# The first down-projection of each feed-forward part moves into the fixed-order region of its round

## The chip, the core and the metric

The kernel runs on one core of a Trainium2 chip. The metric is device time in microseconds (us), as the median of several executions; lower is better. The core has a matrix engine (TensorE, called PE in the profile, with PEld for its weight loads), a vector engine (VectorE, DVE), an activation engine (ScalarE, ACT), GpSimd (POOL), a queue engine that starts transfers (SyncE, SP), and 16 DMA engines. Matrix products accumulate in PSUM, which the kernel uses as eight banks of 128x512 f32. Each engine takes its own instructions in the order in which the program has them, and waits on semaphores for the others.

## The reference

Two layers, each of four parts on a residual stream h of 512 tokens by 1024 channels. The feed-forward part is there twice in a layer, so four times in all:

```
for l in range(DEPTH):                                   # DEPTH = 2
    h = h + 0.5 * swiglu(rms_norm(h, ffn1_norm[l]), w_gate, w_up, w_down)   # first feed-forward part
    h = h + hybrid_mixer(rms_norm(h, mix_norm[l]), ...)  # recurrent + window attention + DeltaNet
    h = h + 0.5 * swiglu(rms_norm(h, ffn2_norm[l]), ...) # second feed-forward part
    h = h + sigmoid(rms_norm(h, ple_norm[l]) @ w_ple_gate[l]) * (p[l] @ w_ple_proj[l])
return rms_norm(h, final_norm)

swiglu(x) = (silu(x @ w_gate) * (x @ w_up)) @ w_down     # 1024 -> 2816 -> 1024
```

All is float32. The change touches the product with w_down, and nothing of what is computed.

## The kernel before, in words

Float32 accuracy is made from three reduced-precision products: every operand is split into a high and a low half, and mm3 (L142 to L145) issues high x high, high x low and low x high as three matmuls of one accumulation. The split of a weight tile (L122 to L125 for down-projection weights, L429 and L434 for gate and up weights) is one ACT instruction that rounds to the high half (gh, wh or sh) and one DVE instruction that subtracts it from the raw tile to get the low half (gl, wl or sl). So each weight tile passes through a DMA on SP's queue into a raw buffer wr (three of them, used in rotation), then ACT, then DVE, then PE.

A feed-forward part is the generator `ffn`. The 2816 hidden channels are 22 blocks of 128, handled as 11 pairs; a pair has a gate unit and an up unit, each a Strassen-like scheme of seven products (class Unit, products p(1) to p(7), L466). Work is in two rounds (ROUNDS): pairs 0 to 4, then 5 to 10. At the end of a round the hidden blocks it made are multiplied with w_down. In round 0 (r == 0) this is the first down-projection: for each of eight output blocks d, `chunk(d)` loads and splits eight of its ten weight blocks, `down` issues 24 matmuls with them, and `end(d)` issues six more with the last two blocks, whose weights `make_end(e)` loads and splits for two values of d at a time, followed by `residual(d)`: two DVE instructions, L566 (dt, scaled from PSUM) and L567 (hT, added to the residual stream). At d = 6 the weights of the first unit of round 1 are prepared too: `pipe[2 * j1].whole()`, which is splits a, b, d, c with the sums s2 (L440) and s4 (L446) between them.

Who sets the order: PE runs in the order of the code everywhere (L73). Inside `with tc.manual_schedule(engines=inner)` (L680, one region in each round), ACT and DVE too run in the order of the code. Outside it, a scheduler with a model of the engines places ACT, DVE and POOL instructions. It may put an instruction ahead of others, also of those of a region before it. SP's transfers and the order of GpSimd follow the scheduler in both versions.

In the kernel before, the units of round 0 are in the region (L680 to L777) and the first down-projection (`if r == 0:`, L779 on) is outside.

Of the kernel before, what the change touches and what calls it, by code (L numbers as in the profile page):

```python
# [19 lines left out]
S = 512  # L20
D = 1024
KD = 8
# [36 lines left out]
def trunk(ctx: ExitStack, tc: tile.TileContext, a):  # L59
# [9 lines left out]
    def bank(shape, name):  # L69
        return banks.tile(shape, F32, tag="b", name=name)  # L70
# [52 lines left out]
    def split(x, hi, lo):  # L123
        A.activation(out=hi, in_=x, func=AF.Copy)  # L124
        V.tensor_tensor(out=lo, in0=x, in1=hi.bitcast(F32), op=ALU.subtract)  # L125
# [16 lines left out]
    def mm3(out, wh, wl, xh, xl, start, stop):  # L142
        T.matmul(out=out, lhsT=wh, rhs=xh, start=start, stop=False)  # L143
        T.matmul(out=out, lhsT=wh, rhs=xl, start=False, stop=False)  # L144
        T.matmul(out=out, lhsT=wl, rhs=xh, start=False, stop=stop)  # L145
# [206 lines left out]
    def ffn(l, which):  # L352
        with ExitStack() as es:
# [23 lines left out]
            def halfgroup():  # L377
                return [fp.tile([128, 4, 128], F32R, tag=t, name=t, bufs=2) for t in ("sh", "sl")]

            def loaded(src, k):  # L380
                raw = wrp.tile([128, k, 128], F32, tag="wr", name="wr")
                nc.sync.dma_start(out=raw, in_=src)
                return raw

            def grouped(raw, k):
                w = group(k, 128)
                split(raw, *w)
                return w


            def load(u):
                j, m = units[u]
                src = a[f"{m}{which}"][l, j]
                if u not in raw1:
                    raw1[u] = loaded(src[:, 0:8], 8)
                    raw3[u] = wrp.tile([128, 8, 128], F32, tag="wr", name="wr")
                    nc.sync.dma_start(out=raw3[u][:, 0:4], in_=src[:, 12:16])

            def load2(u):
                if u < len(units) and u not in raw2:  # L400
                    j, m = units[u]
                    src = a[f"{m}{which}"][l, j]
                    r2 = raw2[u] = fp.tile([128, 8, 128], F32, tag="r2", name="r2", bufs=3)
                    nc.sync.dma_start(out=r2, in_=src[:, 4:12])
                    G.dma_start(out=r2.rearrange("p k n -> p (k n)"), in_=src[:, 8:16].rearrange("p k n -> p (k n)"),
                                accum_op=ALU.add)
# [152 lines left out]
            def down(pd, w, ws, fs, start, stop):  # L559
                for i, f in zip(ws, fs):  # L560
                    h, l_ = (t[:, f % 2, :] for t in hidden[f // 2])
                    mm3(pd, w[0][:, i, :], w[1][:, i, :], h, l_, start and f == fs[0], stop and f == fs[-1])

            def residual(d, pd):
                dt = ft.tile([128, S], F32, tag="ys", name="dt", bufs=2)
                V.scalar_tensor_tensor(out=dt, in0=pd, scalar=0.5, in1=norm.rb, op0=ALU.mult, op1=ALU.mult)  # L566
                V.tensor_tensor(out=hT[:, d, :], in0=hT[:, d, :], in1=dt, op=ALU.add)  # L567
# [3 lines left out]
            pipe = {}  # L571
# [90 lines left out]
            for r, (j0, j1) in enumerate(ROUNDS):  # L662
# [4 lines left out]
                def chunk(d):  # L667
                    if d not in made:
                        made[d] = grouped(loaded(src[l, d][:, t0:t0 + 8, :], 8), 8)
                    return made[d]  # L670

                def make_end(e):
                    raw = wrp.tile([128, 4, 128], F32, tag="wr", name="wr")
                    for i in range(2):
                        nc.sync.dma_start(out=raw[:, 2 * i:2 * i + 2, :], in_=src[l, 2 * e + i][:, 8:10, :])
                    ends[e] = halfgroup()
                    split(raw, *ends[e])

                made, ends = {}, {}
# [96 lines left out]
                    pair.hi()  # L776
                    pair.lo()  # L777

                if r == 0:  # L779
                    def end(d):  # L780
                        e = d // 2
                        if e not in ends:
                            make_end(e)
                        i = 2 * (d % 2)
                        down(pds[d], ends[e], (i, i + 1), (8, 9), False, True)
                        residual(d, pds[d])

                    pds = {}
                    for d in range(KD):
                        pds[d] = bank([128, S], "pd")  # L790
                        chunk(d)
                        if d + 1 < KD:
                            chunk(d + 1)
                        if d == KD - 2:
                            load2(2 * j1)
                            load(2 * j1)
                            pipe[2 * j1] = Weights(2 * j1)
                            pipe[2 * j1].whole()
                        down(pds[d], chunk(d), range(8), range(8), True, False)
                        if d == 0:  # L800
                            continue
                        for e in ((0, 1) if d == 1 else (d,)):
                            end(e)
            pds = []
            for d in range(KD):
                pds.append(bank([128, S], "pd"))
# [796 lines left out]
    norm = Norm(par[:, 0, C_F1:C_F1 + 8], True)  # L1603

    f = ffn(0, 1)
    next(f)
    norm.ps = bank([128, NT, 2], "ssc")
# [18 lines left out]
    for l in range(L):  # L1626
        pl = par[:, l, :]
        norm = rest(f, norm, pl[:, C_MX:C_MX + 8])
        f = ffn(l, 2)
        norm = mixer(l, norm, pl[:, C_F2:C_F2 + 8], f)  # L1630
        norm = rest(f, norm, pl[:, C_PL:C_PL + 8])
        f = ffn(l + 1, 1) if l + 1 < L else None
        norm = ple(l, norm, par[:, l + 1, C_F1:C_F1 + 8] if f else None, f)
# [123 lines left out]
```

## Time and profile before

| what | value |
|---|---|
| median of 3 runs | 2035.08 us (2030.96 to 2036.78) |
| the profiled execution, device time | 2031.3 us |
| its span, first to last instruction | 2029.4 us |
| PE busy | 1978.0 us (97%) |
| DVE, ACT, POOL busy | 1492.6, 980.8, 169.5 us |
| mean granted clock of TensorE | 0.986 |

The profile is of one execution. Busy times are of instructions, so an engine that waits is not busy. The times in rows are microseconds from the start of the span. A row of the timeline has the start, the length (overlapping neighbours in a pipelined engine, so that starts are closer than lengths), the engine, the line of the kernel, the operation, output and inputs, the shape, and in square brackets the idle time before it and what ended it. The granted clock is a share: 1.00 is 2.4 GHz, 0.50 is 1.2 GHz. The names: pd is a PSUM bank of the down-projection, pg, pu, qg and qu are banks of the gate and up units, ys, e, cg, cu and th are temporaries of a unit and its gating, h0h and h0l are the halves of the fifth hidden pair of the round.

### The profile page before, as it was taken

The numbers are of one execution on the slowest core, as the hardware profiler recorded it, in microseconds if no ns is written. First come the engines' busy times: TensorE is split into PE (matmuls) and PEld (weight loads), VectorE is DVE, ScalarE is ACT, GpSimd is POOL, SyncE is SP. The second block draws the span as 40 slices with busy tenths as digits, with TensorE's granted clock in tenths as the row PEclk, the third lists the DMA queues.
The fourth block names the chain that finished last, engine by engine and source line by source line (L and its number), as shares of the span: only waits on it lengthen the run. The fifth ranks groups of instructions, "written<-read, shape, count | busy, mean of one in ns | idle before, by whom it ended". The sixth has DMA issues, their size and how long they took to land.

```text
span 2029.4 us, 32039 instructions
## 1 busy us (share of the span) xinstructions
PE 1978.0 (97%) x12657; PEld 1760.0 (87%) x12657; DVE 1492.6 (74%) x2591; ACT 980.8 (48%) x1629; POOL 169.5 (8%) x182
## 2 busy tenths in 40 slices
PE   8999999999999999999999999999899999999997
PEld 7988998877779989998889899989676899899886
DVE  6875873879868856865788568657887787488466
ACT  5642552455745534643555345434365555155344
POOL 0100000052200000000000000001421000000000
PEclk8999999999999999999999999999999999999998
DMA  6763744221053735645337357423112367275421
GB/s 203 194 169 101 185 120 125 79 73 47 17 161 99 197 121 151 172 123 142 113 101 206 111 146 182 120 88 95 50 35 52 121 161 188 83 189 136 135 71 63
DMA packets 83686, 249.78 MB, mean 123 GB/s; under 512 B 9424, under 2 KB 16848, under 8 KB 83280
## 3 DMA queue, kind: packets, MB, share of 16 engines
q1 hardware_dynamic: 72016, 205.79, 31.7%
q0 software_dynamic: 11520, 41.95, 12.0%
q8 instruction: 99, 1.62, 0.3%
q14 instruction: 51, 0.42, 0.1%
HBM read 245.61 MB, written 2.10 MB: 122 GB/s over the span
## 4 chain that ended last, share of the span: by engine, by line
PE 87%; DVE 7%; ACT 3%; DMA 2%; issue 1%; SPq 0%; POOL 0%; DVEq 0%; ACTq 0%
PE pu L466 10%; PE pg L466 10%; PE pd L143 8%; PE pd L145 8%; PE pd L144 8%; PE qg L466 8%; PE qu L466 7%; PE pp L143 2%; PE pp L144 2%; PE pp L145 2%; PE pg L617 2%; PE pu L617 2%; PE ppg L143 1%; PE ppg L145 1%; PE pwo L145 1%; PE ppg L144 1%
## 5 line engine op out<-in xcount | busy, mean ns | idle before, releaser
L466 PE MATMUL pg<-T,gh 128*128 128x256 f32 x832 | 150.2, 280 | 0.0
L119 ACT ACTIVATE wh<-wr 128x1024 fp32r<-128x1024 f32 (+2 forms) x76 | 77.1, 1015 | 141.7 <-PE pp L144 47.9
L434 DVE TENSOR_TENSOR gl<-wr,gh 128x1024 fp32r<-128x1024 f32 x96 | 117.5, 1224 | 35.3 <-ACT gh L429 35.3
L125 DVE TENSOR_TENSOR gl<-wr,gh 128x1024 fp32r<-128x1024 f32 x56 | 68.6, 1224 | 95.4 <-ACT gh L124 95.3
L466 PE MATMUL pu<-T,gh 128*128 128x256 f32 x736 | 133.2, 280 | 0.0
L466 PEld LDWEIGHTS pg<-T,gh 128*128 128x128 f32 x832 | 127.3, 188 | 0.3
L124 ACT ACTIVATE gh<-wr 128x1024 fp32r<-128x1024 f32 x56 | 59.3, 1059 | 137.6 <-PE pd L144 63.9
L429 ACT ACTIVATE sh<-r 128x512 fp32r<-128x512 f32 x80 | 50.6, 632 | 140.2 <-DVE r L446 140.2
L466 PE MATMUL pg<-T,gl 128*128 128x256 f32 x416 | 116.4, 280 | 0.0
L120 DVE TENSOR_TENSOR wl<-wr,wh 128x1024 fp32r<-128x1024 f32 (+2 forms) x64 | 74.2, 1159 | 54.6 <-ACT wh L119 54.1
L466 PEld LDWEIGHTS pu<-T,gh 128*128 128x128 f32 x736 | 112.3, 188 | 0.0
L429 ACT ACTIVATE gh<-wr 128x1024 fp32r<-128x1024 f32 x96 | 100.6, 1048 | 23.6 <-PE pd L144 23.6
L466 PE MATMUL pu<-T,gl 128*128 128x256 f32 x368 | 102.9, 280 | 0.0
L143 PE MATMUL pp<-X,wh 128*128 128x512 f32 x240 | 101.6, 423 | 0.0
L143 PE MATMUL pd<-X,gh 128*128 128x512 f32 x256 | 101.2, 395 | 0.0
L143 PE MATMUL pd<-X,wh 128*128 128x512 f32 x256 | 101.2, 395 | 0.0
L145 PE MATMUL pd<-X,gl 128*128 128x512 f32 x256 | 100.6, 393 | 0.0
L145 PE MATMUL pd<-X,wl 128*128 128x512 f32 x256 | 100.6, 393 | 0.0
L434 DVE TENSOR_TENSOR gl<-r,gh 128x1024 fp32r<-128x1024 f32 x52 | 63.7, 1224 | 50.0 <-ACT gh L429 50.0
L144 PE MATMUL pd<-X,gh 128*128 128x512 f32 x256 | 100.0, 391 | 0.0
L144 PE MATMUL pd<-X,wh 128*128 128x512 f32 x256 | 100.0, 390 | 0.0
L466 PE MATMUL pu<-T,wh 128*128 128x256 f32 x544 | 98.2, 280 | 0.0
(448 smaller groups left out, 6154.2 us busy)
## 6 DMA issues: line engine op xcount, KB each, us to landing
wr<-in_d_dram SPq DMA_DIRECT2D x64, 512.0 KB, 3.8
wr<-in_g_dram SPq DMA_DIRECT2D x48, 512.0 KB, 4.4
wr<-in_u_dram SPq DMA_DIRECT2D x48, 512.0 KB, 4.0
r<-in_g_dram SPq DMA_DIRECT2D x40, 512.0 KB, 3.9
r<-in_u_dram SPq DMA_DIRECT2D x40, 512.0 KB, 3.9
r<-in_g_dram POOLq DMA_DIRECT2D x40, 512.0 KB, 7.0
r<-in_u_dram POOLq DMA_DIRECT2D x40, 512.0 KB, 6.9
wr<-in_wi_dram SPq DMA_DIRECT2D x30, 512.0 KB, 3.3
```

What stands on the lines that cost most here:

```text
L119: A.activation(out=hi, in_=raw, func=AF.Copy)
L120: (via or V).tensor_tensor(out=lo, in0=raw, in1=hi.bitcast(F32), op=ALU.subtract)
L124: A.activation(out=hi, in_=x, func=AF.Copy)
L125: V.tensor_tensor(out=lo, in0=x, in1=hi.bitcast(F32), op=ALU.subtract)
L143: T.matmul(out=out, lhsT=wh, rhs=xh, start=start, stop=False)
L144: T.matmul(out=out, lhsT=wh, rhs=xl, start=False, stop=False)
L145: T.matmul(out=out, lhsT=wl, rhs=xh, start=False, stop=stop)
L429: A.activation(out=self.g[n][0], in_=self.of(n)[0], func=AF.Copy)
L434: V.tensor_tensor(out=g[1], in0=raw, in1=g[0].bitcast(F32), op=ALU.subtract)
L466: T.matmul(out=ps, lhsT=l_[:, q, :], rhs=r_, start=start and q == 0 and i == 0, stop=stop and q == 3 and i == 2, skip_group_check=more)
L617: T.matmul(out=o[:, cs], lhsT=w_[:, b, :], rhs=x_, start=q + j + n + cs.start == 0, stop=q == 3 and j == 1 and n == 2, skip_group_check=True)
```

## The change

The body of `if r == 0:` is indented by one level, so that it stands inside the region of round 0. No instruction is added or removed; ACT and DVE now run the first down-projection in the order of its code.

```
                     pair.hi()
                     pair.lo()
 
-                if r == 0:
-                    def end(d):
...
-                    pds = {}
-                    for d in range(KD):
...
+                    if r == 0:
+                        def end(d):
+                            e = d // 2
+                            if e not in ends:
+                                make_end(e)
+                            i = 2 * (d % 2)
+                            down(pds[d], ends[e], (i, i + 1), (8, 9), False, True)
+                            residual(d, pds[d])
+
+                        pds = {}
+                        for d in range(KD):
+                            pds[d] = bank([128, S], "pd")
+                            chunk(d)
+                            if d + 1 < KD:
+                                chunk(d + 1)
+                            if d == KD - 2:
+                                load2(2 * j1)
+                                load(2 * j1)
+                                pipe[2 * j1] = Weights(2 * j1)
+                                pipe[2 * j1].whole()
+                            down(pds[d], chunk(d), range(8), range(8), True, False)
+                            if d == 0:
+                                continue
+                            for e in ((0, 1) if d == 1 else (d,)):
+                                end(e)
```

The order of PE, SP and POOL is the same in both kernels; ACT and DVE differ at the four first down-projections, and in a few places of the two mixers, where the scheduler swaps small neighbours. Two places of the first feed-forward part are shown; the other three parts read alike.

First, ACT at the end of round 0's last up unit, before the change. The tile wr_1528 holds chunk 2's raw weights, ys_1440 is the copy of the unit's bank qu, which the product p(4) then adds to, and e_1454 is the copy of its bank pu.

```order
L534 ACTIVATE cu_1399<-pu_1365 128x256
L124 ACTIVATE gh_1530<-wr_1528 128x1024
L539 ACTIVATE ys_1440<-qu_1366 128x512
L543 ACTIVATE e_1454<-pu_1365 128x256
L124 ACTIVATE wh_1456<-wr_1369 128x1024
L124 ACTIVATE sh_1476<-wr_1473 128x512
L124 ACTIVATE gh_1579<-wr_1577 128x1024
```

ACT at the same place after the change, where chunk 2's raw weights are wr_1527.

```order
L534 ACTIVATE cu_1399<-pu_1365 128x256
L539 ACTIVATE ys_1440<-qu_1366 128x512
L543 ACTIVATE e_1454<-pu_1365 128x256
L124 ACTIVATE wh_1456<-wr_1369 128x1024
L124 ACTIVATE sh_1476<-wr_1473 128x512
L481 ACTIVATE th_1494<-cg_1277 128x512 x2
L491 ACTIVATE h0h_185<-th_1494 128x1024
L124 ACTIVATE gh_1529<-wr_1527 128x1024
```

The high half of chunk 2 stood ahead of ys and now stands behind the last gating.

Second, DVE at the end of the first down-projection, before the change: from the residual of d = 4 (hT of dt_1707) to that of d = 6 (dt_1816). sl_1807 is the low half of the end weights for d = 6 and 7; wl_1776 is split c of round 1's first unit.

```order
L567 TENSOR_TENSOR hT_75<-hT_75,dt_1707 128x512
L434 TENSOR_TENSOR sl_1772<-r2_1116,sh_1771 128x512
L434 TENSOR_TENSOR wl_1776<-wr_1759,wh_1775 128x1024
L566 SCALAR_TENSOR_TENSOR dt_1747<-pd_1710,rb_558 128x512
L125 TENSOR_TENSOR sl_1807<-wr_1803,sh_1806 128x512
L440 TENSOR_TENSOR wr_1860<-r2_1241,wr_1858 128x512
L567 TENSOR_TENSOR hT_75<-hT_75,dt_1747 128x512
L566 SCALAR_TENSOR_TENSOR dt_1816<-pd_1750,rb_558 128x512
```

DVE at the same place after the change: the residual of d = 5 (dt_1746), then the low half of chunk 7 (gl_1753), the whole of round 1's first unit (gl_1761 to wl_1775), then the end weights for d = 6 and 7 (sl_1806), and at the end the residual of d = 6.

```order
L566 SCALAR_TENSOR_TENSOR dt_1746<-pd_1709,rb_558 128x512
L567 TENSOR_TENSOR hT_75<-hT_75,dt_1746 128x512
L125 TENSOR_TENSOR gl_1753<-wr_1750,gh_1752 128x1024
L434 TENSOR_TENSOR gl_1761<-wr_1756,gh_1760 128x1024
L440 TENSOR_TENSOR wr_1758<-r2_1116,wr_1756 128x512
L434 TENSOR_TENSOR gl_1766<-r2_1116,gh_1765 128x1024
L446 TENSOR_TENSOR r2_1116<-wr_1758,wr_1756 128x512
L434 TENSOR_TENSOR sl_1771<-r2_1116,sh_1770 128x512
L434 TENSOR_TENSOR wl_1775<-wr_1758,wh_1774 128x1024
L125 TENSOR_TENSOR sl_1806<-wr_1802,sh_1805 128x512
L440 TENSOR_TENSOR wr_1860<-r2_1241,wr_1858 128x512
L566 SCALAR_TENSOR_TENSOR dt_1815<-pd_1749,rb_558 128x512
```

Before, the end weights' split sl_1807 came directly behind the first half of d = 5's residual (dt_1747). Now the second half of that residual and seven instructions more stand between the two.

## Rows read from the trace of the kernel before

**Rows 1.** The page: busy time, share and instructions by engine.
```profile
PE 1978.0 (97%) x12657; PEld 1760.0 (87%) x12657; DVE 1492.6 (74%) x2591; ACT 980.8 (48%) x1629; POOL 169.5 (8%) x182
```

**Rows 2.** Waits of PE, whole span: total us, times, longest.
```profile
PE pk L1227 <- DVE xs L868: 6.7, 2, 3.7
PE qu L466 <- ACT ys L539: 5.5, 6, 1.3
```

**Rows 3.** Window of the first part's first down-projection: us, PE busy, clock, DMA, GB/s.
```profile
120.00:190.00 70.00, 68.89 (x355) 1.00 0.38 109
```

**Rows 4.** Timeline of PE and its weight loads where it waits for ys.
```profile
126.57 0.51 PE L466 MATMUL qu<-T,gh 128*128 128x256 f32 x2 [1.11 <-ACT ys L539]
...
128.10 0.40 PE L466 MATMUL pu<-T,gh 128*128 128x256 f32 x2
...
715.48 0.50 PE L466 MATMUL qu<-T,gh 128*128 128x256 f32 x2 [1.26 <-ACT ys L539]
126.57 0.30 PEld L466 LDWEIGHTS qu<-T,gh 128*128 128x128 f32 x2 [1.31 <-ACT ys L539]
```

**Rows 5.** Timeline of ACT at the first of these waits.
```profile
124.98 1.06 ACT L124 ACTIVATE gh<-wr 128x1024 fp32r<-128x1024 f32 x1 [4.75 <-DMA wr<-in_d_dram]
125.94 0.58 ACT L539 ACTIVATE ys<-qu 128x512 f32<-128x512 f32 x1
```

**Rows 6.** Timeline of PE: start of d = 6, its end weights, start of d = 7.
```profile
171.02 0.40 PE L143 MATMUL pd<-X,wh 128*128 128x512 f32 x1
...
177.02 0.40 PE L145 MATMUL pd<-h0h,sl 128*128 128x512 f32 x1
...
177.94 0.40 PE L143 MATMUL pd<-X,gh 128*128 128x512 f32 x1
```

**Rows 7.** Timeline of DVE in the same stretch.
```profile
170.75 1.22 DVE L434 TENSOR_TENSOR wl<-wr,wh 128x1024 fp32r<-128x1024 f32 x1 [3.15 <-ACT wh L429]
171.89 0.68 DVE L566 SCALAR_TENSOR_TENSOR dt<-pd,rb 128x512 f32<-128x512 f32 x1
172.49 0.68 DVE L125 TENSOR_TENSOR sl<-wr,sh 128x512 fp32r<-128x512 f32 x1
...
178.14 0.69 DVE L566 SCALAR_TENSOR_TENSOR dt<-pd,rb 128x512 f32<-128x512 f32 x1 [3.76 <-PE pd L145]
178.87 0.69 DVE L567 TENSOR_TENSOR hT<-hT,dt 128x512 f32<-128x512 f32 x1
```

**Rows 8.** Timeline of DVE and ACT through s4 and splits of an earlier unit.
```profile
110.77 0.68 DVE L446 TENSOR_TENSOR r<-wr 128x512 f32<-128x512 f32 x1
...
112.15 0.69 DVE L434 TENSOR_TENSOR sl<-r,sh 128x512 fp32r<-128x512 f32 x1
113.10 1.23 DVE L434 TENSOR_TENSOR gl<-wr,gh 128x1024 fp32r<-128x1024 f32 x1 [0.26 <-ACT gh L429]
...
112.02 1.04 ACT L429 ACTIVATE gh<-wr 128x1024 fp32r<-128x1024 f32 x1
```

**Rows 9.** Timeline of SP and ACT: end weights issued, and the split that waits for them.
```profile
129.03 0.80 SPq L675 DMA_DIRECT2D wr<-in_d_dram  x2
132.43 0.63 ACT L124 ACTIVATE sh<-wr 128x512 fp32r<-128x512 f32 x1 [0.58 <-DMA wr<-in_d_dram]
```

**Rows 10.** Timeline of PE: longer waits in the two mixers.
```profile
471.05 0.49 PE L953 MATMUL sc<-T,T 64*128 64x128 f32 x4 [1.54 <-DVE T L1045]
473.90 0.70 PE L953 MATMUL sc<-T,T 64*128 64x128 f32 x4 [1.76 <-DVE mx L957]
1445.95 2.13 PE L1227 MATMUL pk<-kq 64*128 64x256 f32 x8 [3.00 <-DVE xs L868]
```

**Rows 11.** Windows behind such waits: us, PE busy, clock, DMA, GB/s.
```profile
451.00:458.00 7.00, 6.58 (x18) 0.53 0.22 75
474.00:478.00 4.00, 4.00 (x12) 0.57 0.29 89
1447.00:1451.00 4.00, 4.00 (x13) 0.57 0.12 49
```

More of the change, by code (lines that the diff above doesn't have):

```diff
@@ L777, in ffn @@
                     pair.lo()
-                if r == 0:
-                    def end(d):
[L781 to L786, printed above, removed]
-                    pds = {}
-                    for d in range(KD):
[L790 to L803, printed above, removed]
+                    if r == 0:
[22 more added lines that the diff above has]
+                                end(e)
             pds = []
```

## The prediction

> **What bounds the kernel now.** I read the page first: PE is busy 97% of the span, DVE 74%, ACT 48% [rows 1]. Then the windows of the four first down-projections: over 70 us PE is busy 68.89 us at a granted clock of 1.00 in the first, and between 68.74 and 68.83 in the other three [rows 3]. So these stretches are PE's, and any microsecond that PE waits there is a microsecond of the kernel. Then PE's waits over the whole span: the only wait inside a first down-projection or the unit ahead of it is that for ys, 5.5 us in six times [rows 2]. Four of the six, one per feed-forward part, stand at the last up unit of round 0 and take 1.11 to 1.26 us, 4.7 us together [rows 4]; the other two (0.37 us each) stand at the first units and are not touched. ACT's timeline says why: it sat 4.75 us in front of a high half (L124) whose raw weights were still on their way, and ys had to come behind it, at 125.94, although the bank it copies had been ready before [rows 5]. Last I read PE and DVE at d = 6 of the first part [rows 6, 7], because the two orders shown above differ most there.
>
> **The change part by part.** Nothing is added or removed; instructions move on ACT and DVE only. I take the places in order of time.
>
> *ys.* The high half of chunk 2 goes behind the gating, so ACT reaches ys when its bank is ready. PE then goes on without the wait: a gain of 4.7 us in all. It could not be more than 5.5 us [rows 2], nor less than nothing, since nothing new stands ahead of ys.
>
> *The gating and chunks 2 to 5.* h0h and h0l move ahead of the chunks' splits, so they come earlier. Chunk d+1's low half now stands behind the residual of d-1, which PE releases as it begins d. DVE can begin that residual 0.20 us after PE's start of d (178.14 against 177.94) [rows 6, 7], its second half follows 0.73 us later, and each 128x512 instruction passes in 0.60 us, each 128x1024 one in 1.14 us [rows 7]. So a chunk's low half ends some 0.20 + 0.73 + 0.60 + 1.23 = 2.8 us into a block of 6.92 us (171.02 to 177.94) [rows 6] and is needed at the block's end. Where end weights follow (d = 2 and 4) theirs ends at 3.4 us and is needed 6.00 us into the block. Raw buffers are released later too, but still more than a transfer before their use. I take nothing here.
>
> *d = 6.* Call T the start of PE's first matmul of d = 6 (171.02). The end weights' low half is needed by a matmul that stood at 177.02, so at T + 6.00 [rows 6]. Before, DVE made it at 172.49, ahead of T + 2.2 [rows 7]. Now DVE has this in front of it: residual 5 at T + 0.20, its second half at 0.93, chunk 7's low half at 1.53, split a at 2.67, s2 (L440) at 3.81, split b at 4.41, s4 (L446) at 5.55. From s4 on ACT is in the loop, since split d rounds what s4 writes. In an earlier unit s4 began at 110.77, ACT's split after the one of s4's result at 112.02, and DVE's low half of that at 113.10 [rows 8]: so split c's low half begins 2.33 us after s4, at T + 7.88, the end weights' low half 1.14 us later at 9.02, and it ends 0.69 us on, at 9.71. PE took 0.05 us from ys's end (125.94 + 0.58) to the matmul at 126.57 [rows 4, 5], so the matmul starts at T + 9.76 instead of T + 6.00: 3.76 us late, 15.0 us in four parts. Behind the blocked matmul on PE stand the rest of d = 6, all of d = 7, and round 1; none of it has slack to give back, since PE is the bound there.
>
> Bounds: if ACT cost DVE no time in this chain, split d would follow s4 by 0.60 us, and the low half would end at T + 8.58, 2.6 us late. On the other side, the end weights' raw buffer is chunk 7's, free at T + 2.8; an earlier issue took 3.4 us to reach ACT (129.03 to 132.43) [rows 9], so ACT could round at T + 6.2, before its turn at about 7.8. If this took twice as long, the low half would end near T + 10.9, 4.9 us late. I take 3.8, which the nearest rows give.
>
> At the first ys wait the blocked matmul's weight load began with it, at 126.57, and not ahead [rows 4]. The Trainium skill (TensorE: Matmul & The Clock Gate, section "Architectural detail: the array is 16× 32×32, not 1× 128×128") says that PE's queue can pull weight loads ahead of matmuls in flight. By that rule each restart would save a load of some 0.2 us and the time would be about 1 us lower; by the row it saves nothing.
>
> *The clock.* PE would idle about 3 us, then run two matmuls (those that need only the high half, which ACT has ready some 1.3 us sooner), then idle again for most of 1 us. Near such waits the trace shows the granted clock falling to 0.50, the level of 1.2 GHz: after one wait of 3.00 us, after 1.54 and 1.76 us close together [rows 10], and after one of 3.7 us [rows 2]. The windows behind them stand at 0.57, 0.57 and 0.53 [rows 11], so PE lost 4.00 x 0.43 = 1.7 us twice and 6.58 x 0.47 = 3.1 us once. The ys waits, of 1.1 to 1.3 us, were followed by no fall [rows 3]. The new wait is nearest to the 3.00 us one and the pair, so I take 1.7 us each, 6.9 us in four parts. The bounds are nothing and 3.1 us each, 12.4 us.
>
> *The mixers.* A few small DVE and ACT instructions change places with neighbours in both. What moves lies ahead of PE's waits for xs, of which there are two, 3.7 and 3.00 us [rows 2, 10]. If both became like the worse or the better, that is 0.7 us and a difference in clock loss of 1.4 us (3.1 against 1.7): up to 2.1 us either way. I take nothing.
>
> Sum against the profiled execution: 2031.3 + 15.0 - 4.7 + 6.9 = 2048.5 us. That execution was 3.8 us below the median of before, 2035.1; I carry this over and forecast 2052 us.
>
> **The rivals.**
> *The wait is there, but the clock holds.* For it: neither of the two idle pieces is longer than those after which it fell, and the ys waits cost no clock. Against it: the pair of 1.54 and 1.76 us, whose sum is smaller. The time: 2031.3 + 15.0 - 4.7 + 3.8 = 2045.4 us.
>
> *The lateness goes on into round 1.* Behind the end weights DVE now has s2 of round 1's second unit (L440 again), whose raw weights can start only after s4 has freed a buffer, some 11 us later against PE's d = 6 than before. For it: residual 6 and the next splits queue behind that s2. Against it: PE needs that unit's weights only after d = 7 and one whole unit, and is itself 3.8 us later. At 2 us a part this gives 2060 us.
>
> *PE runs on past the blocked matmul.* The 24 matmuls of d = 7 write another bank, have their weights, and take 5.5 us, more than the 3.8 us to be covered. If PE started them, nothing would be lost and only the ys gain would be left: 2031.3 - 4.7 + 3.8 = 2030.4 us, not slower than before. It decides from the point where PE finds 3.8 us of ready work behind a blocked one. Against it: at the ys wait, product p(5) stood ready behind p(4), in another bank, and began at 128.10, only after p(4) [rows 4]. The Trainium skill's reorder window, cited above, is stated for weight loads, and the trace agrees that matmuls do not pass each other.
>
> *The late split is not late,* because DVE finds its way to it as early as before, and the change moves nothing that PE sees beyond a small gain: 2030 to 2035 us. Against it stands the order itself.
>
> **How the numbers follow.** Forecast 0.64, clock holds 0.17, on into round 1 0.10, PE runs past 0.05, not late 0.04. A difference under 0.3%, 6.1 us, cannot be told from no change here. The forecast and the next two cases lie 10 us or more above 2035.1: slower 0.90, leaving a little for small sizes. The last two lie within or just under it: same 0.08, faster 0.02. The range of 2042 to 2061 us reaches from the held clock with a stall at 3 us to the larger clock loss (2031.3 + 15.0 - 4.7 + 12.4 + 3.8 = 2057.8) with the mixers and some of the third case added. It leaves out the last two cases and the rest of the third.
>
> **What would show it.** Right: four waits of PE for the end weights of d = 6 (first for ACT's sh, then for DVE's sl), 3.5 to 4 us together in each part; no wait for ys at the last up unit; clock windows near 0.5 to 0.6 directly behind each new wait; DVE at d = 6 in the order shown, s4 about 5.6 us after PE's start of d = 6. Wrong: no such wait, or one under 2.5 us (then 0.20 + 0.73 and the passing times are wrong); a clock of 1.00 behind it (the first rival); new waits of PE in round 1's first units (the second); PE's d = 7 starting ahead of the end of d = 6 (the third).

## The result, and the profile after

| | before | changed |
|---|---|---|
| median, us | 2033.71 (4 runs, 2030.96 to 2036.78) | 2049.98 (4 runs, 2049.33 to 2053.58) |
| ratio to before | | 1.0079, 95% interval 1.0064 to 1.0095 |
| profiled execution, device time, us | 2031.3 | 2053.58 |
| its span, us | 2029.4 | 2051.6 |
| granted clock, mean | 0.986 | 0.979 |

The changed kernel is slower by 0.8%. Its profiled execution is the slowest of its four and that of the kernel before is 2.4 us below its median, so the spans differ by 22.2 us where the medians differ by 16.3.

PE's waits over the whole span come first, as in [rows 2]: total us, times, longest.

```profile
PE pd L143 <- ACT sh L124: 11.3, 4, 2.8
...
PE pd L145 <- DVE sl L125: 2.2, 4, 0.6
...
PE qu L466 <- ACT ys L539: 0.8, 2, 0.4
```

The four waits for ys of [rows 4] are gone; the two short ones at the first units are left. Two new lines have taken their place, four times each: PE's end matmuls of d = 6 wait for ACT's high half (sh), 2.8 us, and then for DVE's low half (sl), 0.6 us.

The timeline of PE at d = 6 of the first part, to be read beside [rows 6]:

```profile
169.66 0.40 PE L143 MATMUL pd<-X,wh 128*128 128x512 f32 x1
...
174.97 0.40 PE L145 MATMUL pd<-X,wl 128*128 128x512 f32 x1
178.20 0.50 PE L143 MATMUL pd<-h0h,sh 128*128 128x512 f32 x1 [2.83 <-ACT sh L124]
...
179.54 0.79 PE L145 MATMUL pd<-h0h,sl 128*128 128x512 f32 x1 [0.51 <-DVE sl L125]
...
181.41 0.63 PE L143 MATMUL pd<-X,gh 128*128 128x512 f32 x1
181.84 0.63 PE L144 MATMUL pd<-X,gh 128*128 128x512 f32 x1
```

The matmul that needs the low half starts 9.88 us after PE's start of d = 6 (179.54 - 169.66), where it stood at 6.00 before: 3.88 us late. The matmuls behind it are 0.43 us apart in place of 0.23 (181.41 to 181.84).

The timeline of DVE there, beside [rows 7], and of ACT and SP:

```profile
169.86 0.69 DVE L566 SCALAR_TENSOR_TENSOR dt<-pd,rb 128x512 f32<-128x512 f32 x1 [4.37 <-PE pd L145]
170.59 0.69 DVE L567 TENSOR_TENSOR hT<-hT,dt 128x512 f32<-128x512 f32 x1
171.20 1.22 DVE L125 TENSOR_TENSOR gl<-wr,gh 128x1024 fp32r<-128x1024 f32 x1
172.34 1.22 DVE L434 TENSOR_TENSOR gl<-wr,gh 128x1024 fp32r<-128x1024 f32 x1
173.47 0.69 DVE L440 TENSOR_TENSOR wr<-r,wr 128x512 f32<-128x512 f32 x1
174.07 1.22 DVE L434 TENSOR_TENSOR gl<-r,gh 128x1024 fp32r<-128x1024 f32 x1
175.32 0.69 DVE L446 TENSOR_TENSOR r<-wr 128x512 f32<-128x512 f32 x1
176.71 0.69 DVE L434 TENSOR_TENSOR sl<-r,sh 128x512 fp32r<-128x512 f32 x1 [0.70 <-ACT sh L429]
177.66 1.23 DVE L434 TENSOR_TENSOR wl<-wr,wh 128x1024 fp32r<-128x1024 f32 x1 [0.25 <-ACT wh L429]
178.80 0.69 DVE L125 TENSOR_TENSOR sl<-wr,sh 128x512 fp32r<-128x512 f32 x1
```

```profile
176.05 0.63 ACT L429 ACTIVATE sh<-r 128x512 fp32r<-128x512 f32 x1 [10.30 <-DVE r L446]
176.59 1.04 ACT L429 ACTIVATE wh<-wr 128x1024 fp32r<-128x1024 f32 x1
177.53 0.61 ACT L124 ACTIVATE sh<-wr 128x512 fp32r<-128x512 f32 x1
```

```profile
172.45 0.81 SPq L675 DMA_DIRECT2D wr<-in_d_dram  x2
```

DVE is idle for under 1 us between residual 5 and the end weights' low half (the two brackets, 0.70 and 0.25): it works through the queue in front of it. ACT stood idle for 10.30 us until s4 (L446) was written, not until a transfer landed: its three splits follow each other without a gap, and the end weights (issued at 172.45) cost ACT no wait of their own.

Last, windows of 8 us behind the new waits (us, PE busy, clock, DMA, GB/s), beside [rows 11]:

```profile
178.00:186.00 8.00, 7.29 (x18) 0.57 0.77 225
776.00:784.00 8.00, 7.54 (x28) 0.79 0.80 213
1185.00:1193.00 8.00, 7.38 (x19) 0.57 0.90 257
1782.00:1790.00 8.00, 7.38 (x26) 0.79 0.78 217
```

All four hold a stretch at 0.50, long in two and short in two. The cost is read from PE's first matmul of the first down-projection to its first of round 1. In the first part these two stand here, before and then after:

```profile
129.51 0.40 PE L143 MATMUL pd<-X,wh 128*128 128x512 f32 x1
...
184.86 0.40 PE L466 MATMUL pg<-T,gh 128*128 128x256 f32 x2
```

```profile
128.18 0.39 PE L143 MATMUL pd<-X,wh 128*128 128x512 f32 x1
...
190.20 0.40 PE L466 MATMUL pg<-T,gh 128*128 128x256 f32 x2
```

In the four parts this time was 55.32 to 55.35 us before and is 62.02, 60.48, 62.22 and 60.80 us now: 6.67, 5.16, 6.87 and 5.45 us more, 24.2 in all. Of this 4 x 3.88 = 15.5 us is the wait, and the rest, 8.6 us (2.8, 1.3, 3.0, 1.6), comes behind the wait, nearly all of it by the slower clock. In front of these stretches, at the place of ys, PE gains 1.38, 1.52, 1.46 and 1.43 us, 5.8 us in all (in the first part, from the last matmul ahead of ys to the first of the down-projection, 125.18 to 129.51 before and 125.23 to 128.18 after). What is left of the 22.2 us, 3.8 us, lies elsewhere: 3.2 us more in the first layer's mixer, 1.7 us more at the start of layer 2, 1.4 us less in the second mixer, the rest in small pieces. These are differences of the granted clock too. The windows of the first mixer and of the start of layer 2, before and then after:

```profile
420.00:530.00 110.00, 100.67 (x553) 0.95 0.15 49
1018.00:1033.00 15.00, 13.44 (x88) 1.00 0.00 0
```

```profile
425.00:535.00 110.00, 100.78 (x524) 0.92 0.15 49
1030.00:1045.00 15.00, 13.44 (x76) 0.89 0.00 0
```

PE's listed waits in the first mixer's window are 9.0 us before and 9.1 after; the clock takes 110 x 0.05 = 5.5 us there before and 110 x 0.08 = 8.8 after. At the start of layer 2 it takes nothing before and 15 x 0.11 = 1.7 us after.

### The profile page after: what moved, and what is told of

Same layout as the page of the kernel before. It is cut to its first block, busy times and chain, and to the rows that moved or that the text cites. A ratio compares the mean times of both kernels' runs of the same rounds, so it can differ in the third digit from the quotient of the medians.

```text
span 2051.6 us, 32026 instructions
## 1 busy us (share of the span) xinstructions
PE 1990.1 (97%) x12657; PEld 1766.5 (86%) x12657; DVE 1493.1 (73%) x2591; ACT 979.2 (48%) x1629; POOL 168.5 (8%) x182
## 5 line engine op out<-in xcount | busy, mean ns | idle before, releaser
L566 DVE SCALAR_TENSOR_TENSOR dt<-pd,rb 128x512 f32<-128x512 f32 x64 | 44.1, 690 | 97.5 <-PE pd L145 97.5
L145 PE MATMUL pp<-X,wl 128*128 128x512 f32 x240 | 97.9, 408 | 1.1 <-DVE wl L120 1.1
```

## The experiments

Theory A: the change is two independent things, a gain at ys and a larger loss at d = 6, where the end weights' low half stands on DVE (and its high half on ACT) behind seven splits and sums of other work, and the clock falls because PE stands still. Its rivals are named in each expectation. All times are medians of 5 to 8 runs beside runs of the kernel before on the same chip; before was 2031.97 us (9 runs) for the first four and 2033.38 us (13 runs) for the last three.

| run | us | ratio to before, 95% interval |
|---|---|---|
| end weights first | 2024.35 | 0.9958 (0.9943 to 0.9972) |
| d = 7 before the end of d = 6 | 2024.20 | 0.9959 (0.9946 to 0.9971) |
| wait filled with idle matmuls | 2041.78 | 1.0043 (1.0031 to 1.0056) |
| ys behind chunk 2 again | 2055.91 | 1.0120 (1.0100 to 1.0140) |
| end weights after split d | 2039.89 | 1.0033 (1.0022 to 1.0044) |
| before, with only chunk 2 in the region | 2026.30 | 0.9964 (0.9952 to 0.9977) |
| changed again | 2052.25 | 1.0090 (1.0077 to 1.0103) |

**End weights first.**

```
                             if d == KD - 2:
-                                load2(2 * j1)
+                                make_end(3); load2(2 * j1)
```

> The changed kernel, with the end weights for d = 6 and 7 loaded and split at d = 6 before the weights of round 1's first unit instead of behind them. Theory A (the loss is the end weights' low half, queued on DVE behind chunk 7 and seven eighths of a unit's splits): that low half ends about 3.4 us after PE's start of d = 6, where it is needed at 6.0; no wait of PE at d = 6, no fall of the clock there, the gain at ys stays: about 5 us below the kernel before, 2024 to 2031 us, ratio 0.995 to 0.999. Rival B (DVE is too late altogether in this block, whatever stands first: the work pushed behind is missed next, by d = 7 or by round 1's first units): PE waits elsewhere for 2 us or more a part, 2040 us or more.

Measured 2024.35 us. DVE and PE at d = 6 of the first part in this kernel:

```profile
169.07 1.22 DVE L125 TENSOR_TENSOR gl<-wr,gh 128x1024 fp32r<-128x1024 f32 x1
170.21 0.69 DVE L125 TENSOR_TENSOR sl<-wr,sh 128x512 fp32r<-128x512 f32 x1
```

```profile
167.54 0.40 PE L143 MATMUL pd<-X,wh 128*128 128x512 f32 x1
...
173.53 0.40 PE L145 MATMUL pd<-h0h,sl 128*128 128x512 f32 x1
```

The low half ends at 170.90, 3.4 us into the block, and PE uses it at 5.99 with no wait; its list of waits has no line for pd. The work pushed behind is not missed next, which rules out B. Only the order differs (the end weights' load and split stand ahead of the unit's), and 26 to 28 us are saved against the changed kernel's two medians.

**d = 7 before the end of d = 6.**

```
                             down(pds[d], chunk(d), range(8), range(8), True, False)
-                            if d == 0:
+                            if d in (0, KD - 2):
                                 continue
-                            for e in ((0, 1) if d == 1 else (d,)):
+                            for e in ((0, 1) if d == 1 else (d - 1, d) if d == KD - 1 else (d,)):
                                 end(e)
```

> The changed kernel, with PE doing the 24 matmuls of d = 7's chunk before the six end matmuls of d = 6; ACT and SP in the same order as in the changed kernel. Theory A (only the end weights' low half is late, by 3.9 us): it is ready 9.8 us after PE's start of d = 6 and now needed at about 11.5; no wait, 2024 to 2031 us. Rival B (DVE is late for everything in the block): d = 7's chunk comes 5.5 us into the block at the latest, and round 1's first weights follow; a wait at one of them, 2036 us or more. Rival C (the loss is not this wait but something that the region brings elsewhere, in the mixers or in round 1): the time stays within 4 us of the changed kernel's 2050.

Measured 2024.20 us. DVE still makes the end weights' low half as late as in the changed kernel, but PE asks for it later:

```profile
177.13 0.68 DVE L125 TENSOR_TENSOR sl<-wr,sh 128x512 fp32r<-128x512 f32 x1
```

```profile
179.50 0.40 PE L145 MATMUL pd<-h0h,sl 128*128 128x512 f32 x1
```

It ends at 177.81, 1.7 us before its use, and nothing else in the block is missed. So the loss is this one wait and what follows it, not DVE's load and not something that the region does elsewhere: B and C fall.

**The wait filled.**

```
...
                             down(pds[d], chunk(d), range(8), range(8), True, False)
+                            if d == KD - 2:
+                                pds[d + 1] = bank([128, S], "pd")
+                                for i in range(14):
+                                    T.matmul(out=pds[d + 1], lhsT=warm, rhs=warm[:, 0:1].to_broadcast([128, S]), start=True, stop=True)
```

> The changed kernel, with 14 matmuls of zeros (bf16, 128x512, into the bank that d = 7 starts afresh) between d = 6's chunk and its end matmuls on PE: 3.2 us of idle arithmetic that lies inside the wait. Theory A, its part on the clock (PE standing still is what lets the granted clock fall, and that costs 1.3 to 3 us a part, 8.6 us in the profile of the changed kernel): the end matmuls start as late as before, 9.8 to 10 us after PE's start of d = 6, but the clock behind them is 1.00: 2040 to 2045 us. Rival D (the clock falls for another reason, or the fall costs nothing): 2048 to 2052 us, with windows at 0.5 behind the wait as in the changed kernel.

The lines left out keep d = 7 from taking a new bank in place of this one. Measured 2041.78 us, 8 to 10 us below the changed kernel's two medians. PE at d = 6, and windows of 10 us behind the wait in the first and the fourth part:

```profile
175.09 3.22 PE L804 MATMUL pd<-warm 128*128 128x512 bf16 x14
...
179.43 0.50 PE L145 MATMUL pd<-h0h,sl 128*128 128x512 f32 x1 [0.61 <-DVE sl L125]
```

```profile
176.00:186.00 10.00, 9.39 (x42) 1.00 0.73 216
...
1769.00:1779.00 10.00, 9.39 (x42) 1.00 0.67 200
```

The last matmul of d = 6's chunk starts at 174.86 here and at 174.97 in the changed kernel, and the low half's matmul comes 4.57 us after it in both (179.43, 179.54). The time to it is the same to 0.01 us; only the clock behind it is now 1.00. From the first matmul of the down-projection to the first of round 1 PE takes 59.30 to 59.34 us in each part, 15.9 us more than before in all, where the changed kernel takes 24.2 us more. So the clock's share of the loss, 8.2 us, is shown apart from the wait's, and it comes of PE standing still: with the wait filled the clock does not fall.

**ys behind chunk 2 again.** The raw weights of the end blocks and of chunk 2 are issued in the order of the kernel before, and the split of chunk 2 is taken apart:

```
                         unit.p(7)
+                        if not w and r == 0:
...
+                            raw_2 = loaded(src[l, 2][:, t0:t0 + 8, :], 8)
...
+                            A.activation(out=hl_2[0], in_=raw_2, func=AF.Copy)
                         unit.p37()
```

> The changed kernel, with the high half of chunk 2 put ahead of ys on ACT again, as in the kernel before; the end weights and chunk 2 are issued in the same order, the rest is as changed. Theory A, its part on ys (the wait of PE for ys comes from that high half's transfer): four waits for ys of 1.1 to 1.3 us come back, 5 us or a little more: about 2055 us, ratio to before 1.0095 to 1.012. Rival E (the ys wait that went was paid back by the later lateness, or comes from the transfer itself whatever ACT's order): no change, 2048 to 2052 us, ratio 1.007 to 1.009.

Measured 2055.91 us, 5.9 and 3.7 us above the changed kernel's two medians. ACT at the first part, beside [rows 5], and PE's wait:

```profile
125.31 1.06 ACT L742 ACTIVATE gh<-wr 128x1024 fp32r<-128x1024 f32 x1 [5.63 <-DMA wr<-in_d_dram]
126.27 0.58 ACT L539 ACTIVATE ys<-qu 128x512 f32<-128x512 f32 x1
```

```profile
126.90 0.80 PE L466 MATMUL qu<-T,gh 128*128 128x256 f32 x2 [1.99 <-ACT ys L539]
```

The wait is back, and it adds to the loss at d = 6, which stays: the two are independent, and E falls. The size was expected at 1.1 to 1.3 us a wait. This profile was taken in the slowest of the five runs, 9.6 us above their median, and its waits are longer (1.99, 3.20, 1.67 and 2.35 us): in the first part ACT's split begins 0.33 us later than in the kernel before (125.31 against 124.98), and PE stops 0.55 us sooner (its last matmul ahead of ys starts at 124.63 against 125.18). How long the waits are in the other four runs is not shown.

**End weights after split d.** `make_end(3)` is called inside `whole`, between its last two splits:

```
-                def whole(self):
+                def whole(self, mid=lambda: None):
...
-                    self.part("d")
+                    self.part("d"); mid()
...
-                                pipe[2 * j1].whole()
+                                pipe[2 * j1].whole(lambda: make_end(3))
```

> The changed kernel, with the end weights for d = 6 and 7 split between split d and split c of round 1's first unit, so one 128x1024 split less stands in front of them. Theory A: their low half ends 8.3 us after PE's start of d = 6 and is needed at 6.0, so PE waits about 2.4 us a part in place of 3.9 (2 us for the high half, 0.3 to 0.4 for the low half): 6 us below the changed kernel by the wait alone, 2044 us, if the clock falls as often as there; if the shorter wait lets the clock stand, another 8 us less, 2036 us. Rival F (the wait is set by the end weights' transfer, not by DVE's queue): the wait stays at 3.5 us or more, 2048 to 2052 us.

Measured 2039.89 us. The wait, and windows of 7 us behind it in the four parts:

```profile
175.28 0.50 PE L143 MATMUL pd<-h0h,sh 128*128 128x512 f32 x1 [1.89 <-ACT sh L124]
```

```profile
175.00:182.00 7.00, 6.72 (x22) 0.76 0.85 270
771.00:778.00 7.00, 6.29 (x19) 0.76 0.77 261
1178.00:1185.00 7.00, 6.32 (x20) 0.76 0.77 256
1770.00:1777.00 7.00, 6.12 (x25) 1.00 0.80 253
```

The wait is 1.89 us in each of the four parts, and the low half comes without a second wait, which had been put at 0.3 to 0.4 us. So the loss goes down with the work put behind the end weights, as A says, and F falls: the end weights' transfer is issued as late here as in the changed kernel, 2.8 us after PE's start of d = 6 in both. The two cases named for the clock both came: after the same wait it fell in three parts and held in the fourth. From the first matmul of the down-projection to the first of round 1 PE takes 59.23, 59.42 and 59.33 us in the three and 57.87 us in the fourth, so a fall took 1.4 to 1.6 us. The time lies between the two expected, 10 to 12 us below the changed kernel.

**Before, with only chunk 2 in the region.**

```
                     pair.hi()
                     pair.lo()
+                    if r == 0: chunk(2)
                 if r == 0:
```

> The kernel before, with one thing of the change: chunk 2's load and split are issued at the end of the region, so that the scheduler cannot put them ahead of ys; the rest of the first down-projection stays outside, and the end weights of d = 6 are split early as before. Theory A (the change is a gain at ys of about 5 us and a loss at d = 6, independent of each other): no wait for ys at the last up unit, none at d = 6: 2024 to 2030 us, ratio 0.995 to 0.998, as the two versions that take the loss away from the changed kernel. Rival G (the rest of the fixed order gains too, or the scheduler's own order loses once chunk 2 is moved): above 2030 us or below 2022 us.

Measured 2026.30 us. ACT at ys and DVE at d = 6 in the first part:

```profile
124.73 0.60 ACT L539 ACTIVATE ys<-qu 128x512 f32<-128x512 f32 x1 [3.86 <-PE qu L466]
```

```profile
171.12 0.69 DVE L566 SCALAR_TENSOR_TENSOR dt<-pd,rb 128x512 f32<-128x512 f32 x1
171.72 0.68 DVE L125 TENSOR_TENSOR sl<-wr,sh 128x512 fp32r<-128x512 f32 x1
```

ys now waits only for its bank, and the end weights' low half comes directly behind the first half of residual 5, as in [rows 7]. One line takes the change's gain without its loss, 7 us below before. It is as fast as the two repaired versions within what can be told, so G falls. All three gain 7.1 to 7.8 us, more than the 5.8 us at ys; where the rest comes from was not tried.

**Changed again.** The changed kernel itself, unedited.

> The changed kernel itself again, for a second profile and times beside the runs above. Theory A: four waits of 3.8 to 4.0 us at the same place to within 0.1 us, but the length of the stretches at half clock behind them different from those of the first profile (1.3 to 3.0 us lost each), since nothing in the program sets it: 2046 to 2054 us. Rival H (the clock loss is the same at each place in each execution): the same four losses within 0.3 us.

Measured 2052.25 us. Windows of 8 us from a like place in the first and the third part; the second and the fourth stand at 0.79 like the first:

```profile
178.00:186.00 8.00, 7.69 (x28) 0.79 0.77 212
...
1184.00:1192.00 8.00, 7.28 (x18) 0.57 0.73 216
```

PE waits 2.84 us for the high half in each of the four, as in the first profile. Over the same stretches PE took 5.04, 5.32, 6.81 and 5.44 us more than before, so 1.2, 1.4, 2.9 and 1.6 us came behind the wait, nearly all of it by the clock. The first part differs from the first profile (2.8 there); the other three are the same within 0.2 us. So neither A's expectation nor rival H is right as stated: the loss may differ between executions, but at three of four places it did not. What picks the long or the short stretch stays open.

## Why the prediction was right

The forecast was 2052 us in a range of 2042 to 2061, slower, for a wait at d = 6; measured were 2049.98 and, again, 2052.25 us. The mechanism is borne out: the wait stands where it was forecast, for the instructions that were named, and it goes when their order is changed. That the forecast lies within 2.1 us of the median is in part luck, as the last step says. By its steps:

- *ys*: 4.7 us were put down, 5.8 came (1.38 to 1.52 a part), more than the bound of 5.5 us that was taken from [rows 2]. Those rows give idle time, 1.11 us at the first ys; from start to start PE lost 1.27 us there (125.18 to 126.57, where the next matmul else starts 0.12 us on). And the first matmuls after a wait are slower too: in the row at 126.57 two take 0.35 us (to 126.92) where two take 0.23 further on. ACT is at ys at 124.14 now, as soon as its bank is ready, and the experiment that put chunk 2 back showed the cause.
- *The gating and chunks 2 to 5*: nothing, and no wait of PE stands there.
- *d = 6*: the low half was forecast to end 9.71 us after PE's start of d = 6 and ended at 9.83 (178.80 + 0.69 - 169.66). The chain of passing times holds to 0.02 us up to split b; s4 began 1.25 us after that split and not 1.14. With the restart the matmul was 3.88 us late, not 3.76. The bounds were not needed.
- *The clock*: 6.9 us were put down from the nearest rows; 8.6 us came behind the waits in the first profile (8.2 by the run with the wait filled) and 7.1 in the second. The fill shows it to be PE's standing still, and the shorter wait of 1.89 us shows that it need not be as long as the 3 us from which I took the price. The rival with a held clock was right only for one part of that experiment.
- *The mixers*: nothing was put down, with 2.1 us either way. The first layer's mixer cost 3.2 us, the start of layer 2 1.7 us, for which the prediction had no term, and the second mixer gained 1.4 us. This step was too narrow, and it went by PE's waits, which hardly changed; the granted clock did. The moved instructions are not shown to be the cause: two profiles of the changed kernel, with the same order, differ by 1.0 us in the first mixer, at 0.91 in the second profile against 0.92.
- *On into round 1*: no wait of PE came there. In the changed kernel the second unit's s2 began at 179.45 without a wait.
- *PE running past*: it did not. In the changed kernel d = 7's first matmul stands at 181.41, behind all six end matmuls of d = 6, although it was ready. The run that moved d = 7 forward by hand shows that this work would have covered the wait; it took 2024.20 us, below the 2030.4 us that the rival was priced at.
- *From one execution to the median*: against the profile before, the terms came to 15.5 - 5.8 + 8.6 + 3.8 = 22.1 us where 17.2 were forecast. The 3.8 us carried over were added for another reason and happened to make up for most of this; the changed kernel's profiled execution was 3.6 us above its own median, not below it.

## What to carry to other kernels

When work moves from a scheduler's order into the order of the code, look in the new order for instructions that wait for a late event (here a residual that waits for PE) and list what is queued behind them on the same engine and needed soon. Add up the passing times of what stands between, and hold them against the time until use: here eight rows of the trace gave the wait to 0.12 us. A gain and a loss of one edit can often be had apart: one line in the region, or the split that is needed first put first, gave 0.4% where the whole edit lost 0.8%.

## What the runs showed of the hardware that was not expected

PE's wait of 1.89 us at d = 6, followed by matmuls at once, let the granted clock fall in three of four places in one execution and not in the fourth. The length of a wait alone did not decide it. At the start of layer 2 PE waits 0.71 and then 0.84 us in the first profiles of both kernels, and the windows above stand at 1.00 before and 0.89 after. In the profile of ys behind chunk 2 again, the longest of the four ys waits, 3.20 us, has full clock behind it, where those of 1.99 and 2.35 us have a fall (windows at 0.79 and 0.83):

```profile
726.00:736.00 10.00, 7.05 (x42) 1.00 0.27 81
```

The price of one fall came in two sizes, about 1.2 to 1.7 us and about 2.8 to 3.0 us, at waits that were alike to 0.1 us. Fourteen matmuls of zeros, 3.22 us, in the same wait kept the clock at 1.00 in all four places and saved 8.2 us there.
